# A one-core decoder layer: in the first half of the u side, who adds the two halves, who sums the look-up, and how many raw weight buffers there are

## The chip, the cores and the metric

The kernel runs on 1 of the cores of one Trainium2 chip. The metric is device microseconds of an execution, the median of three runs. A profiled execution of the same program gives the trace; its span is the time from the first to the last instruction.

## The reference, cut to what matters

One layer, float32: a mixer of two attention branches, then a PEER feed-forward part, in which each token picks 16 of 16384 single-neuron experts for each of 8 heads.

```python
q = (hf @ wq).reshape(T, PEER_HEADS, 2, PEER_QDIM // 2)          # T = 256 tokens, D = 1024
s = jnp.einsum('thpd,hpnd->thpn', q, subkeys)                    # 128 keys in each of two halves
s1, i1 = lax.top_k(s[:, :, 0], 16); s2, i2 = lax.top_k(s[:, :, 1], 16)
cand = s1[..., :, None] + s2[..., None, :]                       # 256 sums for a token and a head
top_s, pos = lax.top_k(cand, 16)
idx = take_along_axis(i1 * 128 + i2, pos); w = softmax(top_s)
act = gelu(einsum('cd,chkd->chk', x_c, u[idx]))                  # u, v: 16384 x 1024
out = einsum('chk,chkd->cd', w * act, v[idx])
```

The kernel does not gather rows of `u` for most tokens: it multiplies all of `u` with 224 of the 256 tokens (the other 32 are gathered), takes the GELU of everything, and multiplies it later with a weight that is zero for experts that were not picked.

## The kernel before, in words

**Slots.** All large weights pass through one list, `order`, of 128x1024 float32 blocks of 512 KB. Block k is used in slot k. `U0` is written here for the first of the 128 u blocks, and "slot n" below is the n-th of them, counted from 0. The function `slot` writes the instructions of one slot in this order: the fetches (`fetch`, issued by SyncE, SP in the profile), the routing steps of this slot (`first`, below), what stands in the list `early`, the high part of block k + 2 (`whi`, a copy on ScalarE to a shorter float format, L200), its low part (`wlo`, raw minus high, on VectorE, L204), what stands in `late`, the list `pre`, the list `after`, and last the matmuls of block k. Each engine runs its own instructions in just this order; semaphores hold the engines together. There are three buffers each for raw, high and low blocks: the raw buffer of a block comes free when its low part has been taken, and the next transfer into it starts then, whatever slot the other engines are in; a high or low buffer comes free when the matmuls that read it are done.

**The u side, first half.** A pair e is slots 2e and 2e + 1. For pairs 0 to 29 (`WIDE`), `use_both` runs 8 matmuls of 448 columns (high part of the weights times the high and the low part of the tokens, side by side) and 8 of 224 (low part of the weights times the high part of the tokens, added to the second half). The first slot of a pair goes to a bank `pj` of PSUM, the second to a bank `pT`, two buffers of each. So the bank of pair e is wanted again by pair e + 2. The result of a slot is the sum of the two 224-column halves of its bank. Before, ScalarE copies both halves out (`qt`, L1260), GpSimd adds them into `G` (L1261), and ScalarE takes the GELU of the pair one slot later (L1263). In pairs 30 and 31 all matmuls go to one half each and ScalarE takes the GELU straight out of the bank.

**The routing steps.** In the same slots VectorE picks the top 16 keys, builds the candidates, picks again, and looks the chosen indices up. `steps` is a list of steps with a price in us by the author; `advance(PACE)` adds PACE to a credit at the start of a slot and runs steps while the credit lasts. A pick for one head is a step of 0.85 (`top16_a`) and one of 1.25 (`top16_b`). The look-up of one token block b and key half k compares (`look_eq`, L1066), multiplies with a table that ScalarE writes (`look_tab`, L1063; `look_mul`, L1070) and sums 16 products in four halving additions (`look_sum`, L1075; `look_end`, L1080 and L1081). `soft_exp` (L1012) needs another ScalarE table than the GELU. By the prices, block 0 is looked up in slots 28 to 38 before, and block 1 in slots 49 to 59. `tables(1)` in slot 63 transposes the results of block 1 on TensorE; it stands ahead of the matmuls of that slot.

Of the kernel before, what the change touches and what calls it, by code (L numbers as in the profile page):

```python
# [9 lines left out]
F32 = mybir.dt.float32  # L10
# [9 lines left out]
P = 128  # L20
# [8 lines left out]
EPS = 1e-6  # L29
CAND = 112  # L30
TG = 8
PACE = 1.03
WARM = 15
WSCALE = 32768.0
XCUT = ((0, 2), (2, 5), (5, 8))
# [106 lines left out]
def body(tc, nc, a):  # L142
# [31 lines left out]
    order += [a["u_t"][k] for k in range(P)] + [a["v_n"][k] for k in range(P)]  # L174
    raws, parts, at = {}, {}, [0]
    spares, V0, ahead = [], len(order) - P, [3]

    def fetch(k):
        if k in raws or k >= len(order):
            return  # L180
        ap = order[k]
        spare = spares and (k - V0) % (3 + SPARE) >= 3
        t = (spares[0] if spare else stream).tile([P, D], F32, name="raw", **({"bufs": SPARE} if spare else {}))
        if len(ap.shape) == 3:
            t = t[:, :ap.shape[1] * ap.shape[2]]
# [56 lines left out]

    def slot(use, first=(), pre=()):
        k = at[0]
        for n in range(2, ahead[0] + 1):
            fetch(k + n)
        for f in first:
            f()
        run(early)
        new = k + 2 not in parts and k + 2 < len(order)  # L250
        if new:
            high(k + 2)[0]()
        if tick in pre:
# [132 lines left out]
        slot(use, first[1], pre[1])  # L386
        to.append(lambda: evac(box[0]))

    def pair_wide(src, pool, name, sums, done=None, pre=((), ()), bufs=2):
        def use(j):  # L390
            def f(hi, lo):
                o = bank("pj")
                wh, wl = (v.rearrange("p (c m) -> p c m", m=P) for v in (hi, lo))
                for c in range(NC):
                    nc.tensor.matmul(o, wh[:, c], flat(src[:, c]), start=(c == 0), stop=False, skip_group_check=True)  # L395
                for c in range(NC):
                    nc.tensor.matmul(o[:, T:], wl[:, c], src[:, c, 0], start=False, stop=(c == NC - 1),  # L397
                                     skip_group_check=True)

                def out():  # L400
                    t = pool.tile([P, 2, T], F32, name=name, bufs=bufs)
                    nc.scalar.activation(t, halves(o), AF.Copy)
                    nc.gpsimd.tensor_tensor(sums()[:, j], t[:, 0], t[:, 1], OP.add)
                    if j and done:
                        after.append(done)
                early.append(out)
            return f

        slot(use(0), (), pre[0])
        slot(use(1), (), pre[1])  # L410
# [661 lines left out]
    def look_sum(b, k):  # L1072
        e = eq[k]
        for n in (8, 4):
            nc.vector.tensor_tensor(e[:, :, 0:n], e[:, :, 0:n], e[:, :, n:2 * n], OP.add)  # L1075

    def look_end(b, k):
        e = eq[k]
        o = ii[b, k] = sel.tile([P, 8, 16], F32, name="idx", bufs=2)
        nc.vector.tensor_tensor(e[:, :, 0:2], e[:, :, 0:2], e[:, :, 2:4], OP.add)  # L1080
        nc.vector.tensor_tensor(o, e[:, :, 0], e[:, :, 1], OP.add)  # L1081

    def tables(b):
        tp = bank("pO")
# [59 lines left out]
    for b in range(2):  # L1144
        steps.append((1.2, cands, b))
        for m in range(4):
            steps += pick(best, b, m)
            if b == 1 and m == 2:
                steps += [(0.3, route), (0.5, tables, 0)]
        steps += [(0.3, soft_sub, b), (0.9, decode, b), (0.1, soft_exp, b), (1.2, choose, b), (0.2, look_idx, b, 0),  # L1150
                  (1.15, look_eq, b, 0), (0.0, look_tab, b, 0), (0.7, soft_div, b), (0.2, look_idx, b, 1),
                  (1.15, look_mul, b, 0),
                  (1.15, look_eq, b, 1), (0.0, look_tab, b, 1), (0.95, look_sum, b, 0), (0.6, look_end, b, 0), (1.15, look_mul, b, 1),
                  (0.95, look_sum, b, 1), (0.6, look_end, b, 1)]
    credit = [0.0]

    def advance(us):
# [51 lines left out]
    for m in range(8):  # L1209
        first, second = [], []  # L1210
        if m:
            if m + 1 < 8:
                first.append(lambda: sub_load(m + 1))
            if m == 1:
                second.append(lambda: spread(rn2[0], rsb))
            second.append(lambda: score(m - 1))
            second.append(lambda: norm_chunk(m - 1))
            if m == 7:
                second.append(lambda: norm_chunk(7))
            if m > 1:  # L1220
                first.append(lambda m=m: advance(1.6 if 2 < m < 6 else 1.3 if m < 7 else 1.0))
                second.append(lambda: advance(0.6 if m in (2, 7) else 1.4 if m < 6 else 1.2))
        if m in (0, 7):
            pair(q_evac(m), bh, bl, ((), ()), (first, second), last=(6, 7) if m == 0 else (), to=late)
        else:
            pair_wide(bboth, sel, "qt", q_sums(m), pre=([begin_norm] + first if m == 1 else first, second), bufs=3)

    spots = {"blocks": 0, "tokens": 0}  # L1230
    gelus = []
    dense = lambda t: t[:, :2 * TD].rearrange("p (j t) -> p j t", j=2)

    def u_pair(e, first=((), ()), pre=((), ())):
        box = []

        def use(hi, lo):
            j = len(box) and 1
            if not box:
                box.append(bank("pj"))  # L1240
            block_t(box[0][:, j * TD:(j + 1) * TD], (hi, lo), ah[:, :, NG:], al[:, :, NG:])
            box.append(0)
# [24 lines left out]
        def evac():
            g = G[e // 32][:, 2 * (e % 32):2 * (e % 32) + 2]
            w = spots["tokens"]
            pu = dense(box[0])  # L1270
            if w:
                t = oh.tile([P, 2, TD], F32, name="gt", bufs=1)
                nc.scalar.activation(t[:, :, :w], pu[:, :, :w], AF.Gelu)
                if w < TD:
                    nc.scalar.activation(g[:, :, w:], pu[:, :, w:], AF.Gelu)
                gd = g[:, :, :w]
                nc.vector.tensor_tensor(gd, gd, t[:, :, :w], OP.mult)
            else:
                nc.scalar.activation(g, pu, AF.Gelu)
            spots["blocks"] += 2  # L1280

        f = use_both if e < WIDE else use
        if gelus:
            after.append(gelus.pop(0))
        slot(f, first[0], pre[0])
        slot(f, first[1], pre[1])
        if e >= WIDE:
            late.append(evac)

    for e in range(32):  # L1290
        pre = ((rows_out,), (io_tables,)) if e == 0 else ((lambda: score(7),), ()) if e == 1 else ((), ())
# [310 lines left out]
```

## Time and profile before

| | before |
|---|---|
| median of 3 runs | 983.15 us (981.8 to 984.39) |
| profiled execution, its own time | 983.56 us |
| its span | 981.8 us |
| busy share of the span | PE 98%, PEld 92%, DVE 83%, ACT 64%, POOL 23% |
| POOL instructions L1261 (the additions of the halves) | 60, 54.5 us |

PE is TensorE's matmuls and PEld its weight loads, DVE is VectorE, ACT ScalarE, POOL GpSimd. Busy PE is no proof of PE at its peak, since the ends of matmuls are modelled; the distance between the starts of slots tells more. A row of busy time by stretch gives the bounds, the length, busy us and (instructions) of PE, PEld, DVE, ACT and POOL, then the granted TensorE clock, the busy share of the DMA engines, and GB/s. The clock is 1.00 of full speed in all stretches that are shown below.

### The profile page before, as it was taken

Reading aid. Unit: us, or ns where it says so; the run is one execution under the profiler, and the core shown is the slowest. Engines: PE = TensorE matmul, PEld = TensorE weight load, DVE = VectorE, ACT = ScalarE, POOL = GpSimd, SP = SyncE. Lnnn points to the kernel's source line nnn. Section 1 sums busy time; section 2 is a strip of 40 time slices with the busy share of each in tenths; the row PEclk is TensorE's granted clock in tenths of the full one; section 3 lists DMA queues with packets and bytes.
Section 4 is the critical chain, followed back from the end, with each engine's and each line's share of the span. In section 5 each row is a group of like instructions: output and inputs, shape, how many; then the busy total and the mean of one; then the engine's idle time right before and its main releaser. Section 6 shows DMA issues by size and latency. Waiting matters only on the chain.

```text
span 981.8 us, 18999 instructions
## 1 busy us (share of the span) xinstructions
PE 961.0 (98%) x7057; PEld 906.7 (92%) x7057; DVE 810.6 (83%) x1474; ACT 629.7 (64%) x1177; POOL 230.3 (23%) x210
## 2 busy tenths in 40 slices
PE   9999999999999999999999999999999999999996
PEld 7888889999898998889999999999999999999995
DVE  6788876876998979895999999878887888888766
ACT  7556555756576787776988888655555555555563
POOL 3011231001223423331011011114432343334200
PEclk9999999999999999999999999999999999999999
DMA  8823434665556755557665655678888888888871
GB/s 265 273 89 106 122 116 129 181 200 173 178 168 209 225 182 190 188 193 256 210 218 186 212 209 211 203 262 315 319 321 295 288 317 320 317 310 311 284 232 44
DMA packets 61564, 216.63 MB, mean 221 GB/s; under 512 B 7136, under 2 KB 8848, under 8 KB 61464
## 3 DMA queue, kind: packets, MB, share of 16 engines
q1 hardware_dynamic: 48352, 174.42, 53.1%
q0 software_dynamic: 11424, 39.16, 10.9%
q10 hardware_dynamic: 1696, 1.84, 0.6%
q8 instruction: 56, 0.92, 0.4%
q14 instruction: 36, 0.29, 0.1%
HBM read 212.34 MB, written 2.52 MB: 219 GB/s over the span
## 4 chain that ended last, share of the span: by engine, by line
PE 73%; DVE 15%; ACT 5%; DMA 4%; issue 2%; ACTq 0%; SPq 0%; DVEq 0%
PE pj L372 22%; PE acc L1403 21%; PE acc L1407 11%; DVE wlo L204 7%; PE pj L395 4%; PE pw L1350 3%; ACT whi L200 2%; DMA raw<-in_u_t 2%; PE pj L397 2%; PE pT L1252 1%; DMA raw<-in_w_t 1%; PE pj L1252 1%; DVE sc L976 1%; PE pS L689 1%; PE pS L528 1%
## 5 line engine op out<-in xcount | busy, mean ns | idle before, releaser
L204 DVE TENSOR_TENSOR wlo<-raw,whi 128x1024 fp32r<-128x1024 f32 (+2 forms) x329 | 401.9, 1223 | 105.6 <-ACT whi L200 104.6
L200 ACT ACTIVATE whi<-raw 128x1024 fp32r<-128x1024 f32 (+2 forms) x329 | 343.4, 1045 | 73.2 <-DMA raw<-in_u_t 28.5
L1403 PE MATMUL acc<-co,whi 128*128 128x448 f32 x1024 | 231.2, 367 | 0.1
L1403 PEld LDWEIGHTS acc<-co,whi 128*128 128x128 f32 x1024 | 182.9, 189 | 11.7 <-issue 0.3
L372 PE MATMUL pj<-both,whi 128*128 128x224 f32 (+1 forms) x1344 | 170.7, 279 | 1.8 <-ACT whi L200 1.2
L372 PEld LDWEIGHTS pj<-both,whi 128*128 128x128 f32 x1344 | 159.2, 191 | 4.6 <-ACT whi L200 1.6
L1314 ACT ACTIVATE co<-G 128x224 fp32r<-128x224 f32 x128 | 50.0, 391 | 141.3 <-PE acc L1407 141.3
L1407 PEld LDWEIGHTS acc<-co,wlo 128*128 128x128 f32 x1024 | 134.8, 191 | 4.2 <-DVE wlo L204 0.8
L1407 PE MATMUL acc<-co,wlo 128*128 128x224 f32 x1024 | 135.2, 273 | 0.5 <-DVE wlo L204 0.5
L1120 POOL DMA_INDIRECT row<-in_u_n,sidx x32 | 57.1, 1784 | 245.0 <-DVE row L1129 238.5
L372 PE MATMUL pj<-both,wlo 128*128 128x224 f32 (+1 forms) x672 | 90.3, 276 | 0.0
L1120 POOL DMA_INDIRECT row<-in_v_n,sidx x32 | 62.3, 1947 | 106.1 <-DVE ysum L1438 90.0
L372 PEld LDWEIGHTS pj<-both,wlo 128*128 128x128 f32 x672 | 82.8, 191 | 0.0
L1261 POOL TENSOR_TENSOR G<-qt 128x224 f32<-128x224 f32 x60 | 54.5, 913 | 92.0 <-ACT qt L1260 92.0
L1338 ACT ACTIVATE onehot<-onehot,wl 128x128 f16<-128x128 f16 x224 | 71.3, 392 | 7.2 <-DVE onehot L1342 7.1
L1315 DVE TENSOR_TENSOR co<-G,co 128x224 fp32r<-128x224 f32 x128 | 50.4, 394 | 17.3 <-ACT co L1314 17.1
L1252 PE MATMUL pT<-both,whi 128*128 128x448 f32 x240 | 54.6, 369 | 2.8 <-ACT whi L200 2.8
L1252 PE MATMUL pj<-both,whi 128*128 128x448 f32 x240 | 54.6, 370 | 2.1 <-ACT whi L200 1.9
L395 PE MATMUL pj<-both,whi 128*128 128x512 f32 x192 | 51.1, 408 | 0.0
L1252 PEld LDWEIGHTS pT<-both,whi 128*128 128x128 f32 x240 | 42.9, 189 | 6.6 <-ACT whi L200 3.7
L1252 PEld LDWEIGHTS pj<-both,whi 128*128 128x128 f32 x240 | 42.9, 189 | 5.6 <-ACT whi L200 2.6
L395 PEld LDWEIGHTS pj<-both,whi 128*128 128x128 f32 x192 | 34.5, 189 | 7.3 <-issue 0.7
(335 smaller groups left out, 1298.2 us busy)
## 6 DMA issues: line engine op xcount, KB each, us to landing
raw<-in_u_t SPq DMA_DIRECT2D x128, 512.0 KB, 3.3
raw<-in_v_n SPq DMA_DIRECT2D x128, 512.0 KB, 4.0
raw<-in_w_m SPq DMA_DIRECT2D x16, 512.0 KB, 3.7
raw<-in_w_q SPq DMA_DIRECT2D x16, 512.0 KB, 3.6
raw<-in_w_t SPq DMA_DIRECT2D x15, 512.0 KB, 4.8
raw<-in_w_b SPq DMA_DIRECT2D x8, 512.0 KB, 3.5
raw<-in_w_o SPq DMA_DIRECT2D x8, 512.0 KB, 3.6
sg<-in_w SPq DMA_DIRECT2D x4, 512.0 KB, 6.5
```

What stands on the lines that cost most here:

```text
L200: return [lambda s=slice(u, min(v, n)): nc.scalar.activation(hi[:, s], raws[k][:, s], AF.Copy) for u, v in cuts]
L204: nc.vector.tensor_tensor(lo[:, cs], raws[k][:, cs], hi[:, cs].bitcast(F32), OP.subtract)
L372: nc.tensor.matmul(out, (wl if v == 2 else wh)[:, c], (l if v == 1 else h)[:, c], start=(i == 0), stop=(i == len(seq) - 1))
L395: nc.tensor.matmul(o, wh[:, c], flat(src[:, c]), start=(c == 0), stop=False, skip_group_check=True)
L1120: nc.gpsimd.indirect_dma_start(rows_of_step(n), None, src, bass.IndirectOffsetOnAxis(ap=sidx[:, n % NG:n % NG + 1], axis=0))
L1252: nc.tensor.matmul(o[:, :2 * TD], wh[:, c], both[:, c, :, NG:], start=(c == 0), stop=False, skip_group_check=True)
L1261: nc.gpsimd.tensor_tensor(g[:, j], t[:, 0], t[:, 1], OP.add)
L1314: nc.scalar.activation(t[:, :TD], g, AF.Copy)
L1315: nc.vector.tensor_tensor(t[:, TD:], g, t[:, :TD].bitcast(F32), OP.subtract)
L1338: nc.scalar.activation(E[:, 1, t], E[:, 1, t], AF.Copy, scale=wl[:, n:n + 1])
L1403: nc.tensor.matmul(acc[c][:, :2 * TD], w[0][:, c * P:(c + 1) * P], coefs[k], start=(k == 0), stop=False, skip_group_check=True)
L1407: nc.tensor.matmul(acc[c][:, small], w[1][:, c * P:(c + 1) * P], coefs[k][:, :TD], start=False, stop=(k == P - 1), skip_group_check=True)
```

## The change

Four things in the first half of the u side. The copies on ScalarE take only the second halves (224 columns of each bank, tile `lowsum`), both at the start of the slot after the pair, and VectorE adds them to the first halves, which it reads out of the banks; the GELU follows in the slot after that. The four additions of a look-up go from VectorE to GpSimd, and are priced 0.05 and 0.05 instead of 0.95 and 0.6. PACE is 0.92 instead of 1.03. From block `U0 + 8` to the end of the half, two blocks of every five go to two further raw buffers, which lie in SBUF that is no longer used (half of `xt`, and `g_wide`), and fetches are written up to five blocks ahead. The tile `qt` of the stage before has two buffers instead of three.

```diff
-PACE = 1.03
+PACE = 0.92
...
+    U0, UM = V0 - P, V0 - P // 2
+    more = []
...
+        other = more and U0 + 8 <= k < UM and (k - U0) % (3 + SPARE) >= 3
+        t = more[(k - U0) % (3 + SPARE) - 3] if other else (spares[0] if spare else stream).tile(...
...
-        for n in range(2, ahead[0] + 1):
-            fetch(k + n)
+        far = 3 + SPARE if U0 + 4 <= k < UM else ahead[0]
+        for n in range(2, far + 1):
+            if n <= 3 or not k < UM <= k + n:
+                fetch(k + n)
...
     def look_sum(b, k):
         e = eq[k]
         for n in (8, 4):
-            nc.vector.tensor_tensor(e[:, :, 0:n], e[:, :, 0:n], e[:, :, n:2 * n], OP.add)
+            nc.gpsimd.tensor_tensor(e[:, :, 0:n], e[:, :, 0:n], e[:, :, n:2 * n], OP.add)
...
-            def out():
-                t = sel.tile([P, 2, T], F32, name="qt", bufs=3)[:, :, :TD]
-                nc.scalar.activation(t, dense(o), AF.Copy)
-                nc.gpsimd.tensor_tensor(g[:, j], t[:, 0], t[:, 1], OP.add)
-                if j:
-                    gelus.append(lambda: nc.scalar.activation(g, g, AF.Gelu))
-                    spots["blocks"] += 2
-            early.append(out)
+        def evac_both():
+            g = G[e // 32][:, 2 * (e % 32):2 * (e % 32) + 2]
+            t = sel.tile([P, 2, TD], F32, name="lowsum", bufs=2)
+            for j in range(2):
+                nc.scalar.activation(t[:, j], box[j][:, TD:2 * TD], AF.Copy)
+
+            def add():
+                for j in range(2):
+                    nc.vector.tensor_tensor(g[:, j], t[:, j], box[j][:, :TD], OP.add)
+                late.append(lambda: nc.scalar.activation(g, g, AF.Gelu))
+            after.append(add)
+            spots["blocks"] += 2
```

On VectorE, slots 1 to 4 of the u side hold this before (`tv`, `ti` and `sc` are the values, indices and scores of a pick; the lines of a program are counted anew in each kernel, so L204 before is L207 after):

```order
L204 TENSOR_TENSOR wlo<-raw,whi 128x1024
L970 MAX tv_2696<-sc 128x8 x2
L972 MAX_INDEX ti_2698<-tv_2696,sc 128x8 x2
L204 TENSOR_TENSOR wlo<-raw,whi 128x1024
L976 MATCH_REPLACE sc<-tv_2696,sc 128x128 x2
L978 MAX tv_2696<-sc 128x8 x2
L980 MAX_INDEX ti_2698<-tv_2696,sc 128x8 x2
L204 TENSOR_TENSOR wlo<-raw,whi 128x1024
```

and this after, the two additions (L1267) behind the low part of the second slot of a row, and no step in slot 3:

```order
L207 TENSOR_TENSOR wlo<-raw,whi 128x1024
L975 MAX tv_2696<-sc 128x8 x2
L977 MAX_INDEX ti_2698<-tv_2696,sc 128x8 x2
L207 TENSOR_TENSOR wlo<-raw,whi 128x1024
L1267 TENSOR_TENSOR G_2674<-lowsum,pj 128x224
L1267 TENSOR_TENSOR G_2674<-lowsum,pT 128x224
L207 TENSOR_TENSOR wlo<-raw,whi 128x1024
```

What moved: in every even slot from 2 on, the bank of the pair before is given back only when VectorE has passed its steps and the low part of the block two slots ahead.

The second place is VectorE in the look-up of block 0, from the product for key half 0 on, before (slots 33 to 36):

```order
L1070 TENSOR_TENSOR sc<-sc 128x2048
L204 TENSOR_TENSOR wlo<-raw,whi 128x1024
L1066 TENSOR_TENSOR sc<-ab_4294,io_2677 128x2048
L204 TENSOR_TENSOR wlo<-raw,whi 128x1024
L1075 TENSOR_TENSOR sc<-sc 128x8x128
L1075 TENSOR_TENSOR sc<-sc 128x8x64
L1080 TENSOR_TENSOR sc<-sc 128x8x32
L1081 TENSOR_TENSOR idx<-sc 128x128
L204 TENSOR_TENSOR wlo<-raw,whi 128x1024
```

and after (slots 37 to 40; the product is L1075 here and the comparison L1071, and `xg` and `g_wide` are the two further raw buffers):

```order
L1075 TENSOR_TENSOR sc<-sc 128x2048
L207 TENSOR_TENSOR wlo<-g_wide,whi 128x1024
L1071 TENSOR_TENSOR sc<-ab_4375,io_2677 128x2048
L207 TENSOR_TENSOR wlo<-raw,whi 128x1024
L1267 TENSOR_TENSOR G_2674<-lowsum,pj 128x224
L1267 TENSOR_TENSOR G_2674<-lowsum,pT 128x224
L1075 TENSOR_TENSOR sc<-sc 128x2048
L207 TENSOR_TENSOR wlo<-raw,whi 128x1024 x2
L1267 TENSOR_TENSOR G_2674<-lowsum,pj 128x224
```

What moved: the four additions are gone from here, and the additions of the halves have come. On GpSimd the 60 additions of the halves are gone, and the look-up of block 0 stands there twice four deep, each addition waiting for the one above it:

```order
L1080 TENSOR_TENSOR sc<-sc 128x8x128
L1080 TENSOR_TENSOR sc<-sc 128x8x64
L1085 TENSOR_TENSOR sc<-sc 128x8x32
L1086 TENSOR_TENSOR idx<-sc 128x128
L1080 TENSOR_TENSOR sc<-sc 128x8x128
L1080 TENSOR_TENSOR sc<-sc 128x8x64
L1085 TENSOR_TENSOR sc<-sc 128x8x32
L1086 TENSOR_TENSOR idx<-sc 128x128
```

What moved: the first of each four starts as soon as VectorE has made the product, without waiting for a slot. By the prices, block 0 is now looked up in slots 31 to 39 and block 1 in slots 52 to 60.

## Rows read from the trace of the kernel before

**Rows 1.** Busy time by stretch; bounds are starts of slots 2, 14, 30, 41, 50, 60.

```profile
280.93:313.67 32.74, 30.87 (x195) 28.98 (x194) 29.17 (x109) 21.68 (x32) 11.91 (x16) 1.00 0.62 203
313.67:354.05 40.38, 40.38 (x258) 38.37 (x257) 35.45 (x130) 29.55 (x46) 16.31 (x16) 1.00 0.70 220
354.05:384.71 30.66, 29.15 (x178) 26.35 (x177) 27.21 (x35) 24.61 (x37) 11.36 (x12) 1.00 0.54 174
384.71:407.74 23.03, 23.03 (x149) 21.90 (x148) 23.03 (x81) 15.58 (x26) 7.71 (x12) 1.00 0.69 228
407.74:437.10 29.36, 26.55 (x162) 23.96 (x161) 22.61 (x30) 25.52 (x41) 10.27 (x11) 1.00 0.49 162
```

**Rows 2.** Timeline of PE: start, us, what, idle before and releaser.

```profile
303.71 1.80 PE L1252 MATMUL pT<-both,whi 128*128 128x448 f32 x8
...
308.10 1.90 PE L1252 MATMUL pj<-both,whi 128*128 128x448 f32 x8 [1.70 <-ACT whi L200]
...
457.21 2.04 PE L372 MATMUL pj<-both,whi 128*128 128x224 f32 x16 [0.86 <-ACT whi L200]
```

**Rows 3.** Chain that ended last: start, us, what; around slot 12.

```profile
301.34 8.52 DMA raw<-in_u_t
309.94 1.07 ACT whi L200
```

**Rows 4.** The same chain in the picks: steps and low parts on DVE.

```profile
291.48 0.53 DVE sc L976 x3
...
292.92 1.12 DVE wlo L204
294.05 0.39 DVE tv L970 x2
...
294.97 1.55 DVE wlo L204
```

**Rows 5.** Timeline of DVE at the end: additions with one input in PSUM.

```profile
966.64 0.39 DVE L1522 TENSOR_TENSOR last<-acc,x 128x224 f32<-128x224 f32 x1
966.95 0.38 DVE L1521 TENSOR_TENSOR x<-x,acc 128x224 f32<-128x224 f32 x1
```

**Rows 6.** Groups by shape, DVE, 275 to 440 us: busy us, mean ns.

```profile
L1075 DVE TENSOR_TENSOR sc<-sc 128x1024 bf16<-128x1024 bf16 x4 | 4.6, 1157 | 0.0
L1075 DVE TENSOR_TENSOR sc<-sc 128x512 bf16<-128x512 bf16 x4 | 2.7, 676 | 0.1
L1080 DVE TENSOR_TENSOR sc<-sc 128x256 bf16<-128x256 bf16 x4 | 2.1, 524 | 0.1
L1081 DVE TENSOR_TENSOR idx<-sc 128x128 f32<-128x128 bf16 x4 | 1.2, 292 | 0.1
```

**Rows 7.** ACT: a chain row (start, us), then groups by shape (busy us, mean ns).

```profile
349.80 0.52 ACT f L1032 x3
...
L1012 ACT ACT_TABLE_LOAD x2 | 2.6, 1283 | 0.0
...
L1063 ACT ACTIVATE sc<-tib 128x1024 bf16<-128x1024 bf16 x8 | 8.0, 1047 | 2.5 <-DVE sc L1070 2.5
...
L1260 ACT ACTIVATE qt<-pT 128x448 f32<-128x448 f32 x30 | 16.1, 536 | 6.9 <-PE pT L1255 4.7 <-POOL G L1261 2.2
```

**Rows 8.** POOL and DVE side by side: two timeline rows, then lines (min/median/max ns).

```profile
102.53 2.12 POOL L706 TENSOR_TENSOR y<-y,ytmp 128x512 f32<-128x512 f32 x1 [1.37 <-DVE ytmp L705]
...
103.44 1.36 DVE L629 TENSOR_SCALAR cleft<-csb,ka 128x256 fp32r<-128x256 f32 x1
...
L1066 DVE TENSOR_TENSOR sc<-ab,io x4: 1210/1213/1221, 360.0 to 425.8; 128x2048 bf16<-128x2048 bf16 x4
...
L1070 DVE TENSOR_TENSOR sc<-sc x4: 1687/1690/1702, 365.5 to 433.2; 128x2048 bf16<-128x2048 bf16 x4
```

**Rows 9.** Lines of POOL: durations, ns min/median/max.

```profile
L1261 POOL TENSOR_TENSOR G<-qt x60: 659/674/3428, 282.4 to 438.2; 128x224 f32<-128x224 f32 x60
...
L706 POOL TENSOR_TENSOR y<-y,ytmp x4: 1282/1707/2128, 99.9 to 137.7; 128x512 f32<-128x512 f32 x4
```

More of the change, by code (lines that the diff above doesn't have):

```diff
@@ L182, in fetch @@
         spare = spares and (k - V0) % (3 + SPARE) >= 3
-        t = (spares[0] if spare else stream).tile([P, D], F32, name="raw", **({"bufs": SPARE} if spare else {}))
+        other = more and U0 + 8 <= k < UM and (k - U0) % (3 + SPARE) >= 3
+        t = more[(k - U0) % (3 + SPARE) - 3] if other else (spares[0] if spare else stream).tile([P, D], F32, name="raw", **({"bufs": SPARE} if spare else {}))
         if len(ap.shape) == 3:
@@ L387, in pair, with pair_wide @@
         to.append(lambda: evac(box[0]))
-    def pair_wide(src, pool, name, sums, done=None, pre=((), ()), bufs=2):
+    def pair_wide(src, pool, name, sums, done=None, pre=((), ())):
         def use(j):
@@ L400, in out @@
                 def out():
-                    t = pool.tile([P, 2, T], F32, name=name, bufs=bufs)
+                    t = pool.tile([P, 2, T], F32, name=name, bufs=2)
                     nc.scalar.activation(t, halves(o), AF.Copy)
@@ L1079, in look_end @@
         o = ii[b, k] = sel.tile([P, 8, 16], F32, name="idx", bufs=2)
-        nc.vector.tensor_tensor(e[:, :, 0:2], e[:, :, 0:2], e[:, :, 2:4], OP.add)
-        nc.vector.tensor_tensor(o, e[:, :, 0], e[:, :, 1], OP.add)
+        nc.gpsimd.tensor_tensor(e[:, :, 0:2], e[:, :, 0:2], e[:, :, 2:4], OP.add)
+        nc.gpsimd.tensor_tensor(o, e[:, :, 0], e[:, :, 1], OP.add)
     def tables(b):
@@ L1152, in body @@
                   (1.15, look_mul, b, 0),
-                  (1.15, look_eq, b, 1), (0.0, look_tab, b, 1), (0.95, look_sum, b, 0), (0.6, look_end, b, 0), (1.15, look_mul, b, 1),
-                  (0.95, look_sum, b, 1), (0.6, look_end, b, 1)]
+                  (1.15, look_eq, b, 1), (0.0, look_tab, b, 1), (0.05, look_sum, b, 0), (0.05, look_end, b, 0), (1.15, look_mul, b, 1),
+                  (0.05, look_sum, b, 1), (0.05, look_end, b, 1)]
     credit = [0.0]
@@ L1225, in body @@
         else:
-            pair_wide(bboth, sel, "qt", q_sums(m), pre=([begin_norm] + first if m == 1 else first, second), bufs=3)
+            pair_wide(bboth, sel, "qt", q_sums(m), pre=([begin_norm] + first if m == 1 else first, second))
     spots = {"blocks": 0, "tokens": 0}
-    gelus = []
     dense = lambda t: t[:, :2 * TD].rearrange("p (j t) -> p j t", j=2)
@@ L1242, in use @@
             box.append(0)
-        g = G[e // 32][:, 2 * (e % 32):2 * (e % 32) + 2]
         def use_both(hi, lo):
-            j = len(box)
-            o = bank("pT" if j else "pj")
+            o = bank("pT" if box else "pj")
             box.append(o)
@@ L1282, in u_pair @@
         f = use_both if e < WIDE else use
-        if gelus:
-            after.append(gelus.pop(0))
         slot(f, first[0], pre[0])
         slot(f, first[1], pre[1])
-        if e >= WIDE:
-            late.append(evac)
+        (early if e < WIDE else late).append(evac_both if e < WIDE else evac)
     for e in range(32):
+        if e == 2:
+            more += [flat(xt[:, 0:4]), g_wide]
         pre = ((rows_out,), (io_tables,)) if e == 0 else ((lambda: score(7),), ()) if e == 1 else ((), ())
```

## The prediction

> **What bounds the kernel now.** I read first the busy time by stretch, cut at the starts of slots [rows 1], then the timeline of TensorE around the gaps [rows 2], and last the chain of waits there [rows 3]. In the second stretch 16 slots take 40.38 us, 2.524 us each, with PE busy throughout: that is the pace which the matmuls set. Against it the first stretch (12 slots) loses 32.74 - 30.29 = 2.45 us, the third (11 slots, the look-up of block 0) 30.66 - 27.76 = 2.90, the fourth (9 slots) 0.31, and the fifth (10 slots, the look-up of block 1) 29.36 - 25.24 = 4.12. So there are 9.8 us to be had in this half, and none beyond it but 0.86 us in slot 67, where PE waits for a high part [rows 2]. The loss of the first stretch is one event: slot 11 starts at 303.71 and slot 12 at 308.10, since a transfer that is 2 to 3 slots ahead at best took 8.52 us [rows 3]. In the look-ups the columns of DVE and ACT say more than PE's: DVE is busy for 27.21 of 30.66 us and ACT for 25.52 of 29.36; in the picks between them DVE is busy for all 23.03 us [rows 1]. What the reader is to see: PE sets the pace, VectorE is just behind it, and the look-ups, where VectorE and ScalarE wait for each other, are where time is lost.
>
> **Raw buffers.** With five buffers a transfer may start when the low part five blocks back is taken instead of three back, two slots or 5.0 us sooner, and the stall of slots 12 and 13 came from a transfer about 5 us too slow for its place. I take the whole 2.45 us. At the end of the half the buffers rotate so that the blocks of slots 64 to 66 start a slot sooner, which should free slot 67: 0.86 us. Term -3.3; at least -2.4, if only the first holds.
>
> **Additions on VectorE in the picks.** A step of 0.85 takes 294.97 - 294.05 less the low part before it; between the starts of the rows the low part stands for 1.13 us, the short step for 0.92 and the long one for 1.44 [rows 4]. So 2.1 credits cost 2.36 us, 1.12 us a credit. Before, a slot gives VectorE 1.03 x 1.12 + 1.13 = 2.29 us. An addition with one input in a bank stands for 0.31 us when the next follows at once and for 0.39 alone [rows 5]; there is one a slot. After: 0.92 x 1.12 + 1.13 + 0.31 = 2.47 us, or 2.55 at the upper end. Against 2.524 of PE that is 0 to +1.0 us over 37 slots of picks. Term +0.3. GpSimd's 60 additions, which lay beside other work, go for nothing.
>
> What this does to the slack matters more. In slot 6 the low part starts at 294.97 and ends near 296.5 [rows 4], while slot 7 starts about 293.6 (280.93 and five slots): VectorE is 2.9 us late. Before, it wins back 0.23 us a slot; at slot 28, which starts near 349.0, ScalarE already copies the decoded positions at 349.80 [rows 7], only 0.8 us late. After, it wins back 0.05 us a slot, so it comes to the look-up in slot 31 about 2 us late. And the bank of pair e is given back behind the low part of its slot, so the same lateness stands between TensorE and the start of pair e + 2.
>
> **The look-up of block 0, after.** On ScalarE, from the start of slot 31: 2.0 late, 0.3 for the first decoding, 0.9 for five copies (three take 0.52 [rows 7]), a high part of 1.07 [rows 3], GELU and exponential about 0.9 (an estimate), a table load of 1.28, two copies of 0.37 (half of 0.536 at least, all of it at most [rows 7]), a high part of 1.07: 8.3 us, where slot 34 needs it at 7.57. Then index, high part, table load, GELU, two table copies of 1.05 [rows 7], two half copies, high part: 7.0 us for two slots of 5.05. Together 2.7 us lost. Then the product (slot 37) must be followed by the table for the second key half (2.0), two copies (0.74), the high part (1.07), the low part (1.13) and one addition (0.31), 5.25 us, before slot 40 can start. VectorE is then between 1.0 us late (copies, high part, low part and additions, 3.56, less a slot) and 3.3 (nothing won back); with 2.7, and 1.3 for the product, slot 40 comes 1.7 us late and slot 38 about 0.5: 2.2.
>
> **The sums on GpSimd.** No sum of this kind ran there. By the additions of 224 (0.659) and 512 elements (1.282) [rows 9], 2.16 ns an element: 2.39, 1.28, 0.73 and 0.45 us, 4.85 for a chain; half of that, or twice, are the bounds, since these are 2-byte numbers. Two rows say that GpSimd and VectorE shut each other out. An operation of VectorE's on 256 elements took 1.36 us, more than the low part's 1.13 for 1024, and ended at 104.80, just after GpSimd's 2.12 us had ended at 104.65 [rows 8]. And all four products took 1.69 us where the comparison of the same size took 1.21 [rows 8]; in each case an addition of GpSimd's had been waiting and went first. But GpSimd also lost: one of its 0.66 us additions took 3.43 [rows 9]. The Trainium skill, "SBUF — State Buffer", section "Who interferes with whom", states that a VectorE operation with two inputs in SBUF and a GpSimd operation that reads SBUF exclude each other for a whole instruction, whoever issues first. By that rule, each chain would cost its length; by the 3.43 us, VectorE can go on past a waiting GpSimd and pay less. I take what lies between: behind the low part the first sum (2.39) gets in before the comparison, and VectorE loses 2.1; in the second chain low parts follow one another, 1.5. In block 1 the first chain costs 2.1; the second runs in slots 60 to 63, where no additions stand on VectorE, and only `tables(1)` waits for it, 0 to 3.7, taken as 0.9.
>
> What goes: 10.6 us of sums from VectorE (4.6 + 2.7 + 2.1 + 1.2 [rows 6]). They are left out of the chains above, so nothing is subtracted again.
>
> **Sum.** Look-up of block 0: 2.7 + 2.2 + 2.1 + 1.5 = 8.5 us against 2.90, +5.6. Block 1, where decoding and exponential fall in one slot and VectorE is as late: 1.9 + 1.7 + 2.1 + 0.9 = 6.6 against 4.12, +2.5. With -3.3 and +0.3 that is +5.1. On the profiled execution's own 983.56 (span 981.8) it gives 988.7; the median of the runs is 0.4 lower, so **988.3 us**.
>
> **The rivals.** (A) Faster. VectorE catches up after all, because nothing of GpSimd's gets in its way in the picks, and ScalarE, which has 0.17 us a slot less to copy, never falls behind; the look-ups then lose about 1.5 and 2.0 us. For it: ScalarE has idle time in the picks (29.55 of 40.38 busy [rows 1]), and sums on VectorE are part of today's loss. Against it: 2.47 of 2.524 leaves almost nothing to win back with. It gives -1.4 - 2.1 - 3.3 = -6.8, about 976.4. It decides where an addition costs VectorE under 0.25 us net. (B) No change to be measured: the sums give way on GpSimd, as in the 3.43 us, and the rest holds: 4.9 and 3.6 us in the look-ups, +2.0 - 0.5 + 0.3 - 3.3 = -1.5, 981.7. (C) Every sum shuts VectorE out, 4.2 us a chain (4.85 less what passes under two additions), and `tables(1)` waits 3.7: 4.9 + 8.4 = 13.3 and 3.6 + 4.2 + 3.7 = 11.5 us, +10.4 + 7.4 - 3.0, 998. The page named above would have it so; the products that all lost 0.48 speak for it, the 3.43 us against it.
>
> **How the numbers follow.** The forecast has 0.40 (its own range 985.5 to 993), A 0.29, B 0.20, C 0.11. A range from 977 to 997 leaves out about 0.13 below, the lower half of A, and 0.06 above. A difference of 0.3%, 2.9 us, is about what a measurement of this kernel tells from none. Faster than that: A, 0.29. Within it: most of B and the edge of the forecast, 0.20. Slower: the rest, 0.51.
>
> **What would show it.** Right: no wait of ScalarE for raw blocks around slot 12; VectorE over 95% busy in slots 14 to 30; PE waiting for the additions L1267 or for high parts in slots 33 to 44 and 53 to 60; comparisons or low parts of 2.5 us and more beside a GpSimd sum. Wrong: starts of slots 2.53 us apart through the look-ups, or sums on GpSimd under 1 us. If the picks themselves run at over 2.6 us a slot, an addition costs more than rows 5 show, and the loss is larger and elsewhere.

## The result, and the profile after

Predicted 988.3 us (977 to 997); measured 990.32 us (median of 4, 989.67 to 991.42), against 983.19 us (981.8 to 984.39) for the kernel before on the same chip. The ratio is 1.0076, 95% interval [1.0061, 1.0092]: slower, as forecast, by 7.1 us. The profiled execution took 990.62 us, its span is 988.8.

First the busy time by stretch, cut at the starts of slots 2, 14, 30, 41, 50, 60 and 67 (columns as in [rows 1]):

```profile
279.86:314.24 34.38, 31.17 (x195) 29.11 (x194) 30.25 (x112) 19.85 (x32) 1.61 (x3) 1.00 0.71 239
314.24:354.62 40.38, 40.38 (x259) 38.35 (x257) 39.87 (x142) 25.34 (x40) 0.00 (x0) 1.00 0.66 216
354.62:386.52 31.90, 28.43 (x178) 26.57 (x177) 26.71 (x51) 24.67 (x42) 9.03 (x5) 1.00 0.53 170
386.52:411.50 24.98, 23.48 (x149) 22.04 (x148) 24.98 (x78) 13.78 (x26) 6.75 (x6) 1.00 0.57 191
411.50:441.04 29.54, 25.62 (x163) 24.05 (x161) 25.09 (x49) 22.52 (x38) 7.93 (x5) 1.00 0.50 162
441.04:464.49 23.45, 21.00 (x172) 20.77 (x172) 16.34 (x16) 13.02 (x25) 11.96 (x9) 0.93 0.65 220
```

Against [rows 1]: the picks (second row) run at the same 40.38 us, with VectorE busy for 39.87 of them. The first stretch, where five buffers should have saved 2.4 us, is 1.6 us longer. The look-up of block 0 (third row) is 1.2 longer, the stretch behind it 1.95, the look-up of block 1 0.2, and the seven slots behind that 3.3 (20.11 before: from 437.10 [rows 1] to 457.21 [rows 2]). These are 8.4 us. The half starts 1.1 us sooner (279.86 for 280.93), ahead of the new steps of the u side, and 0.3 are won behind slot 67 (524.3 us to the end of the span for 524.6); so the span is 7.0 longer.

The timeline of TensorE shows where the slots wait:

```profile
294.67 1.90 PE L1253 MATMUL pT<-both,whi 128*128 128x448 f32 x8 [1.77 <-ACT whi L203]
298.88 1.46 PE L1253 MATMUL pj<-both,whi 128*128 128x448 f32 x6 [1.43 <-DVE G L1267]
...
383.94 1.86 PE L1253 MATMUL pj<-both,whi 128*128 128x448 f32 x8 [1.64 <-DVE G L1267]
...
423.58 1.86 PE L1253 MATMUL pj<-both,whi 128*128 128x448 f32 x8 [1.82 <-DVE G L1267]
441.04 2.02 PE L377 MATMUL pj<-both,whi 128*128 128x224 f32 x16 [2.10 <-DVE G L1267]
451.98 0.33 PE L1091 MATMUL pO<-ident,idx 128*128 128x128 f32 x1 [2.44 <-POOL idx L1086]
```

Three kinds of wait: a raw block with what follows from it (slots 7 and 8, at 294.67 and 298.88; the stall of slots 12 and 13 is gone), the additions L1267 that give the bank back (slots 34, 36, 40, 42, 44, 54 and 60, of which three are shown), and in slot 63 the index that GpSimd's last sum makes.

The chain of waits around slot 7 (start, us, what), and GpSimd's issue of the copy that sends 32 token rows to all groups (`tokens_out`):

```profile
284.67 8.49 DMA raw<-in_u_t
...
293.56 1.06 ACT whi L203
...
294.64 1.23 DVE wlo L207
```

```profile
283.70 0.61 POOL L1115 DMA_DIRECT2D xhs<-xhd  x1 [2.36 <-DMA xhd<-xhw]
```

Before, the same copy stands 14 us later, since GpSimd had the additions of the halves ahead of it in its queue:

```profile
297.64 0.64 POOL L1110 DMA_DIRECT2D xhs<-xhd  x1
```

The 8.52 us transfer of [rows 3], at 301.34, came behind it. So the slow transfer has moved along with the copy; whether the copy is its cause is what e2, e4 and e5 ask.

VectorE in the look-up of block 0, from its product for key half 0 on:

```profile
375.95 1.22 DVE L1075 TENSOR_TENSOR sc<-sc 128x2048 bf16<-128x2048 bf16 x1
377.09 1.22 DVE L207 TENSOR_TENSOR wlo<-g_wide,whi 128x1024 fp32r<-128x1024 f32 x1
378.22 3.17 DVE L1071 TENSOR_TENSOR sc<-ab,io 128x2048 bf16<-128x2048 bf16 x1
381.31 2.18 DVE L207 TENSOR_TENSOR wlo<-raw,whi 128x1024 fp32r<-128x1024 f32 x1
...
385.15 4.53 DVE L207 TENSOR_TENSOR wlo<-raw,whi 128x1024 fp32r<-128x1024 f32 x2
```

and GpSimd beside it:

```profile
377.26 5.15 POOL L1080 TENSOR_TENSOR sc<-sc 128x1024 bf16<-128x1024 bf16 x2 [92.95 <-DVE sc L1075]
...
385.47 5.22 POOL L1080 TENSOR_TENSOR sc<-sc 128x1024 bf16<-128x1024 bf16 x2
```

The comparison of 1.21 us [rows 8] stands for 3.17, two low parts for 4.53 instead of 2.3, and the bank that slot 40 waits for is free 1.64 us late.

Last the end of the half by stretch: slot 62 with the wait at its end, then slots 63 and 64 (the clock is third from the end):

```profile
446.46:452.06 5.60, 3.15 (x29) 2.92 (x28) 5.18 (x3) 2.02 (x3) 5.37 (x5) 1.00 0.38 117
452.06:456.08 4.02, 4.02 (x25) 4.02 (x26) 0.29 (x1) 0.94 (x3) 2.42 (x3) 0.67 0.90 324
456.08:459.12 3.04, 3.04 (x25) 3.04 (x25) 1.28 (x2) 2.18 (x3) 0.00 (x0) 0.88 0.91 333
```

Behind the wait the granted clock is 0.67 and 0.88 of full speed: part of each slot ran at 1.2 GHz instead of 2.4. Slots 63 and 64 take 7.06 us, where the two slots behind them take 5.37 (459.12 to 464.49).

### The profile page after: what moved, and what is told of

It reads as the page before. It is cut to its first block, busy times and chain, and to the rows that moved or that the text cites. A ratio compares the mean times of both kernels' runs of the same rounds, so it can differ in the third digit from the quotient of the medians.

```text
span 988.8 us, 18941 instructions
## 1 busy us (share of the span) xinstructions
PE 961.7 (97%) x7057; PEld 908.7 (92%) x7057; DVE 822.3 (83%) x1518; ACT 619.3 (63%) x1177; POOL 207.1 (21%) x166
## 3 DMA queue, kind: packets, MB, share of 16 engines
HBM read 212.34 MB, written 2.52 MB: 217 GB/s over the span
## 4 chain that ended last, share of the span: by engine, by line
PE 83%; DVE 10%; ACT 3%; issue 1%; DMA 1%; POOL 1%; SPq 0%; DVEq 0%; ACTq 0%; POOLq 0%
PE pj L377 25%; PE acc L1407 21%; PE acc L1411 11%; PE pj L400 4%; DVE wlo L207 4%; PE pj L1253 4%; PE pT L1253 3%; PE pw L1354 3%; PE pj L402 2%; PE pj L1256 2%; PE pT L1256 2%; ACT whi L203 1%; PE pS L694 1%; DMA raw<-in_u_t 1%; PE pS L533 1%
## 5 line engine op out<-in xcount | busy, mean ns | idle before, releaser
L207 DVE TENSOR_TENSOR wlo<-raw,whi 128x1024 fp32r<-128x1024 f32 (+2 forms) x306 | 376.2, 1231 | 90.7 <-ACT whi L203 89.8
L203 ACT ACTIVATE whi<-raw 128x1024 fp32r<-128x1024 f32 (+2 forms) x306 | 318.6, 1044 | 56.2 <-PE pj L377 28.9
L1080 POOL TENSOR_TENSOR sc<-sc 128x1024 bf16<-128x1024 bf16 (+1 forms) x8 | 20.4, 2548 | 114.9 <-DVE sc L1075 114.6
```

What stands on the lines that cost most here:

```text
L203: return [lambda s=slice(u, min(v, n)): nc.scalar.activation(hi[:, s], raws[k][:, s], AF.Copy) for u, v in cuts]
L207: nc.vector.tensor_tensor(lo[:, cs], raws[k][:, cs], hi[:, cs].bitcast(F32), OP.subtract)
```

## The experiments

The theories: the sums on GpSimd cost most, because GpSimd and VectorE shut each other out and because `tables(1)` waits for the last chain; and the buffers gain nothing because the copy now starts early. The rivals: that the additions on VectorE are what costs; and that the burst of fetches with which five buffers begin makes the stall. Each run was timed beside the kernel before on its own chip: 982.3 to 982.8 us on the three chips of the runs, 983.19 on the chip of the changed kernel. So times of different runs compare to about 1 us.

Losses in the table are the length of a stretch less 2.524 us for each of its slots, from the starts of slots in each trace; the last column is the plain length. A trace is of one execution: that of e4 is the fastest of six (985.1 to 989.76 us), and a stretch in which the granted clock fell, as told at the end, is longer by that.

| kernel | us | slots 2-14 | 30-41 | 41-50 | 50-60 | 60-67, us |
|---|---|---|---|---|---|---|
| before | 983.2 | 2.45 | 2.90 | 0.31 | 4.12 | 20.11 |
| after | 990.3 | 4.09 | 4.14 | 2.26 | 4.30 | 23.45 |
| e1: after, sums on VectorE | 984.25 | 4.41 | 2.96 | 1.11 | 3.61 | 19.60 |
| e2: before, five buffers | 979.07 | 0.06 | 2.89 | 0.32 | 4.12 | 19.08 |
| e3: before, sums on GpSimd | 994.29 | 2.77 | 1.81 | 6.55 | 2.27 | 26.66 |
| e4: after, copy later | 986.86 | 0.73 | 4.17 | 2.26 | 4.81 | 21.83 |
| e5: after, three buffers | 990.66 | 4.20 | 4.17 | 2.26 | 4.91 | 24.90 |
| e6: after, last chain on VectorE | 987.15 | 3.99 | 4.16 | 2.27 | 4.30 | 19.86 |
| e7: e1 and e4 together | 979.65 | 0.99 | 2.94 | 1.11 | 3.10 | 19.63 |
| e8: e2, halves on VectorE in look-ups | 978.13 | 0.06 | 3.46 | 0.32 | 3.04 | 19.09 |
| e9: e5 with e1, idle sums on GpSimd | 995.6 | 4.28 | 8.30 | 1.95 | 6.22 | 22.48 |
| e10: e8 in block 1 alone | 977.56 | 0.07 | 2.91 | 0.32 | 3.16 | 19.08 |

### e1: the sums on VectorE again

```diff
-            nc.gpsimd.tensor_tensor(e[:, :, 0:n], e[:, :, 0:n], e[:, :, n:2 * n], OP.add)
+            nc.vector.tensor_tensor(e[:, :, 0:n], e[:, :, 0:n], e[:, :, n:2 * n], OP.add)
...
-        nc.gpsimd.tensor_tensor(e[:, :, 0:2], e[:, :, 0:2], e[:, :, 2:4], OP.add)
-        nc.gpsimd.tensor_tensor(o, e[:, :, 0], e[:, :, 1], OP.add)
+        nc.vector.tensor_tensor(e[:, :, 0:2], e[:, :, 0:2], e[:, :, 2:4], OP.add)
+        nc.vector.tensor_tensor(o, e[:, :, 0], e[:, :, 1], OP.add)
```

> The changed kernel, with the four look-up sums issued on VectorE again; their prices in the step list, the pace and their place in the order stay as in the changed kernel. Theory (the sums on GpSimd cost through the exclusion of VectorE and through the late last chain): the comparisons of 3.17 us and low parts of 4.53 us for two go back to about 1.2 each, slot 63 no longer waits 2.4 us for idx, and the clock does not fall in slots 63 and 64; VectorE gets 10.6 us of sums back, of which the exclusion cost about as much. About 4 to 6 us faster than the changed kernel, 985 +-1.5. Rival (VectorE is the bound of the look-ups because of the additions): the 10.6 us of sums stand on its path, the waits for the additions grow, and the kernel takes 992 or more.

984.25 us, ratio to before 1.0014 [1.0005, 1.0023]: 6.1 us faster than the changed kernel. Groups by shape on VectorE, 275 to 470 us (busy us, mean ns):

```profile
L1071 DVE TENSOR_TENSOR sc<-ab,io 128x2048 bf16<-128x2048 bf16 x4 | 4.9, 1216 | 0.0
L1080 DVE TENSOR_TENSOR sc<-sc 128x1024 bf16<-128x1024 bf16 x4 | 2.7, 687 | 0.1
L1080 DVE TENSOR_TENSOR sc<-sc 128x512 bf16<-128x512 bf16 x4 | 1.7, 427 | 0.1
L1085 DVE TENSOR_TENSOR sc<-sc 128x256 bf16<-128x256 bf16 x4 | 1.2, 292 | 0.1
L1086 DVE TENSOR_TENSOR idx<-sc 128x128 f32<-128x128 bf16 x4 | 1.2, 291 | 0.1
```

The 16 sums take VectorE 6.8 us in all; in [rows 6] they took 10.6, with GpSimd's additions running beside them. And in the changed kernel the four comparisons alone stand for 8.8 us instead of 4.9, and 58 low parts have means of 1.33 to 1.35 us instead of 1.21 to 1.22, 7 us more in all:

```profile
L207 DVE TENSOR_TENSOR wlo<-raw,whi 128x1024 fp32r<-128x1024 f32 x46 | 61.2, 1334 | 12.1 <-ACT whi L203 12.0
L207 DVE TENSOR_TENSOR wlo<-xg,whi 128x1024 fp32r<-128x1024 f32 x12 | 16.2, 1349 | 2.5 <-ACT whi L203 2.4
...
L1071 DVE TENSOR_TENSOR sc<-ab,io 128x2048 bf16<-128x2048 bf16 x4 | 8.8, 2193 | 0.0
```

So VectorE was relieved of 6.8 us, and its comparisons and low parts stood for some 11 longer.

### e2: the five raw buffers alone

The edits of `fetch`, `slot`, `U0`, `UM` and `more` from the change, put into the kernel before.

> The kernel before, with the five raw buffers alone (additions of halves on GpSimd, sums on VectorE). Theory (the stall of slots 7 and 8 in the changed kernel is there because GpSimd's queue reaches the copy of the tokens 14 us sooner): the copy still starts near 297.6, when five buffers are in use, so slots 12 and 13 lose nothing and slot 67 too; 2.5 to 3.3 us faster than before, 980.3 +-1. Rival (the burst of three fetches when the two new buffers are taken up makes the stall by itself): slots 7 and 8 lose about 4 us here as well, and the time is 983 to 985.

979.07 us, ratio 0.9962 [0.9949, 0.9976]: 3.3 us faster, the size that the prediction gave this term. The first stretch loses nothing, and slots 60 to 67 are 1.0 us shorter:

```profile
279.20:309.55 30.35, 30.35 (x195) 28.83 (x194) 30.35 (x109) 22.00 (x32) 13.56 (x16) 1.00 0.75 255
...
432.98:452.06 19.08, 19.08 (x173) 19.08 (x172) 13.52 (x15) 12.61 (x23) 4.34 (x4) 1.00 0.78 260
```

The copy stands at 295.91 here, behind GpSimd's additions:

```profile
295.91 0.64 POOL L1115 DMA_DIRECT2D xhs<-xhd  x1
```

### e4: the copy of the tokens later

```diff
     def tokens_out():
-        nc.gpsimd.dma_start(xhs.rearrange("(g t) d -> g t d", t=NG), xhd[None].to_broadcast([NR, NG, D]))
+        nc.sync.dma_start(xhs.rearrange("(g t) d -> g t d", t=NG), xhd[None].to_broadcast([NR, NG, D]))
```

> The changed kernel, with the copy of the tokens (L1115) issued from SyncE's queue behind the fetch of block 13 instead of from GpSimd's, where nothing holds it. Theory (the early copy slows the fetches while only three buffers are in use): the copy starts near 298 us, no raw block of slots 7 and 8 takes over 5 us, and the 4.1 us lost in slots 2 to 14 go: about 986.3. Rival (the burst of fetches itself is the cause): slots 7 and 8 still lose about 4 us and the time stays at 990.

986.86 us, ratio 1.0044 [1.0028, 1.0060]: 3.5 us faster than the changed kernel. On SyncE's queue the burst of fetches begins at 284.02 with the first of the two further buffers (`xg`), 1.03 us before its place in the changed kernel, as slot 2 does (278.81 for 279.86); the copy follows at 294.42, and slots 2 to 14 lose 0.73 us instead of 4.09:

```profile
284.02 0.42 SPq L192 DMA_DIRECT2D xg<-in_u_t  x1
...
294.42 0.72 SPq L1115 DMA_DIRECT2D xhs<-xhd  x1
```

### e5: the early copy with three buffers

The changed kernel without the edits of e2.

> The changed kernel with three raw buffers, as before: no burst of three fetches, but the copy of the tokens still issued early, at about 283 us, by GpSimd. Theory (the copy by itself slows the fetches, whatever is in flight): a raw block of slots 6 to 9 still comes about 2 to 4 us late, slots 12 and 13 lose nothing, slot 67 loses its 0.9 again, and the time is 990 to 992. Rival (only copy and burst together are too much): no stall in slots 2 to 14 at all, 986 to 988.

990.66 us, ratio 1.0091 [1.0076, 1.0107]. No burst, the copy at 282.71, and the stall is there in slots 7 and 8 as in the changed kernel, behind a transfer of the same length (chain of waits):

```profile
283.74 8.59 DMA raw<-in_u_t
```

With e4 this settles it for the changed kernel: the early copy from GpSimd's queue makes the stall, with the burst or without. Where five buffers are in use when the copy starts, there is none, from SyncE's queue (e4) or from GpSimd's (e2); an early copy from SyncE's queue was not run. That the stall of slots 12 and 13 before came from the copy too fits this. In e3, again with three buffers, the copy stands at 295.77, a block's transfer takes 8.84 us from 296.93 on, and slot 12 starts 2.6 us late. But no run took the copy out of such a kernel. One expectation failed: slot 67 does not lose 0.9 us again here, it starts 2.68 us behind slot 66. And in the changed kernel the five buffers, worth 3.3 us by themselves, are worth nothing that the times resolve (990.3 and 990.7).

### e6: the last chain on VectorE

```diff
-            nc.gpsimd.tensor_tensor(e[:, :, 0:n], e[:, :, 0:n], e[:, :, n:2 * n], OP.add)
+            (nc.vector if (b, k) == (1, 1) else nc.gpsimd).tensor_tensor(e[:, :, 0:n], e[:, :, 0:n], e[:, :, n:2 * n], OP.add)
```

and likewise for the two additions of `look_end`.

> The changed kernel with the last of the four chains of sums (block 1, second key half) on VectorE, the other three on GpSimd. Theory (tables(1) waits 2.4 us for the GpSimd chain, and the clock falls behind that wait): slot 63 starts 2.7 us after slot 62, slots 63 and 64 keep their full clock: 3 to 4.5 us faster than the changed kernel, 986 to 987. Rival (the chain is late because VectorE is late with its product, so the wait stays, and the clock falls at another stall): less than 1.5 us faster, 989 or more.

987.15 us, ratio 1.0058 [1.0044, 1.0072]: 3.2 us faster than the changed kernel by the medians, but only 1.8 by the ratios, whose intervals overlap. The traces are clearer: slots 60 to 67 take 19.86 us instead of 23.45, and no other stretch of the table moves by more than 0.1. Slot 63 starts 3.00 us behind slot 62 (447.06 to 450.06), and the clock in it stays at 1.00:

```profile
450.06:452.81 2.75, 2.75 (x27) 2.75 (x26) 1.43 (x2) 1.10 (x4) 2.02 (x2) 1.00 0.84 289
```

So that chain costs 3.6 us by the traces, about half of what the sums cost: from e1 to the changed kernel slots 30 to 60 lose 3.0 us more, and slots 60 to 67 are 3.85 longer.

### e9: sums that nobody waits for

In the changed kernel with three raw buffers and the sums on VectorE, GpSimd does four additions of the same sizes a chain beside them (`look_sum` calls `idle_sum` first), into a tile that nobody reads.

```diff
+    def idle_sum(k, b):
+        e = eq[k]
+        d = g_wide.bitcast(BF).rearrange("p (h a k) -> p h a k", h=8, a=16)
+        nc.gpsimd.tensor_tensor(d[:, :, 0:8], e[:, :, 8:16], e[:, :, 8:16], OP.add)
+        nc.gpsimd.tensor_tensor(d[:, :, 0:4], d[:, :, 0:4], d[:, :, 4:8], OP.add)
+        nc.gpsimd.tensor_tensor(d[:, :, 0:2], d[:, :, 0:2], d[:, :, 2:4], OP.add)
+        nc.gpsimd.tensor_tensor(d[:, :, 8], d[:, :, 0], d[:, :, 1], OP.add)
```

> The changed kernel with three raw buffers and its sums on VectorE, and beside them the same four additions a chain on GpSimd as work that nobody waits for: they read a half of the comparison that nothing writes, and write into a tile that this half does not use. Their results are thrown away. So GpSimd is on no path, and only its sharing with VectorE can cost. Theory (exclusion): the comparison behind the first product takes 3.2 us again, low parts 2.2 us and more, and the stretches 30-41, 41-50 and 50-60 lose 2 to 5 us more than the 2.96, 1.11 and 3.61 of the kernel with the sums on VectorE alone; slot 63 keeps its 2.7 to 3.0. Rival (sums on GpSimd cost because of who waits for them): the comparison takes 1.2 us and the stretches lose what they lost there, within 1 us in all.

995.6 us, ratio 1.0135 [1.0116, 1.0155]. On VectorE, at the comparison and the sums that stand beside the first of them:

```profile
377.43 1.22 DVE L204 TENSOR_TENSOR wlo<-raw,whi 128x1024 fp32r<-128x1024 f32 x1
378.56 2.92 DVE L1066 TENSOR_TENSOR sc<-ab,io 128x2048 bf16<-128x2048 bf16 x1
381.40 2.46 DVE L1084 TENSOR_TENSOR sc<-sc 128x1024 bf16<-128x1024 bf16 x2
```

and GpSimd:

```profile
377.60 2.80 POOL L1075 TENSOR_TENSOR g_wide<-sc 128x1024 bf16<-128x1024 bf16 x1 [93.31 <-DVE sc L1070]
...
387.65 2.31 POOL L1075 TENSOR_TENSOR g_wide<-sc 128x1024 bf16<-128x1024 bf16 x1 [3.51 <-DVE sc L1070]
390.04 1.23 POOL L1076 TENSOR_TENSOR g_wide<-g_wide 128x512 bf16<-128x512 bf16 x1
```

GpSimd's sum ends at 380.40 and the comparison 1.08 us behind it, about its own length of 1.22; it takes 2.92 us. VectorE's own sums, with GpSimd's additions beside them, take 15.3 us where they take 6.8 in e1. The low parts, expected at 2.2 us and more, are not longer (mean 1.216 us): in this kernel VectorE's sums stand where low parts do in the changed one. The three stretches of the look-ups lose 8.8 us more than in e1 (16.47 less 7.68), above the 2 to 5 expected. Part of that is the slower clock behind the waits: slot 40 takes 4.81 us at a clock of 0.50, and slot 41 4.10 at 0.83; but e1 pays for one such slot too (slot 54, 4.17 at 0.59). So the two engines' sharing costs by itself, with no engine waiting for GpSimd's results. That it costs the 6 to 7 us of the change in just the same way is argued from this and the comparisons above.

### e3: the sums on GpSimd, alone

The edits of `look_sum`, `look_end`, the prices and PACE, in the kernel before.

> The kernel before, with the four look-up sums on GpSimd alone (and their prices and the pace as in the changed kernel). Theory (each sum shuts VectorE out for its own length, and tables(1) waits for the last chain): comparisons of about 3.2 us and slot 63 late by 2 to 3 us, 3 to 6 us slower than before, 986 to 989. Rival (the sums off VectorE free it, and only together with the additions of halves on VectorE do they hurt): 2 to 4 us faster than before, 979 to 981.

994.29 us, ratio 1.0117 [1.0098, 1.0135]: 11.95 us slower, where 3 to 6 were expected. GpSimd still has the additions of the halves in its queue, behind the sums, and ScalarE waits for them:

```profile
384.54 0.58 ACT L1263 ACTIVATE G<-G 128x448 f32<-128x448 f32 x1 [3.15 <-POOL G L1261]
...
392.14 0.55 ACT L1260 ACTIVATE qt<-pT 128x448 f32<-128x448 f32 x1 [5.65 <-POOL G L1261]
```

With ScalarE held for 5.65 us no high part is made, and slots 43 and 44 take 6.15 and 4.68 us, the second at a clock of 0.52. `tables(1)` waits 4.67 us, since the last chain stands behind two additions of the halves. By these waits the sums hurt less in the change than alone because the additions had left GpSimd.

### e7, e8, e10: the rest of the account

e7 is the changed kernel with the edits of e1 and e4: five buffers and the halves on VectorE remain, with the new pace and prices, which were not run by themselves.

> The changed kernel without its sums on GpSimd (they are issued on VectorE) and with the copy of the tokens issued from SyncE's queue: what remains of the change is five raw buffers and the halves added on VectorE. If the account is additive (sums -6.1, copy -3.5 on the changed kernel's 990.3): 980.7 +-1.2, which leaves +1.6 for the halves on VectorE beside the five buffers alone. Rival (the halves on VectorE cost what the prediction put on lateness, about +4 in the look-ups once the sums are on VectorE as well): 983 or more.

979.65 us, ratio 0.9973 [0.9964, 0.9982], 0.6 us above the five buffers alone, with intervals that overlap: the halves on VectorE cost nothing that these runs resolve. The three look-up stretches lose 7.15 us, and 7.33 with the halves on GpSimd (e2).

e8 and e10 ask whether the halves do better on VectorE in the look-ups alone.

```diff
+    LOOK = lambda e: 15 <= e < 21 or 25 <= e < WIDE
...
+            if LOOK(e):
+                return
...
+        elif LOOK(e):
+            early.append(evac_both)
```

> The kernel before with five raw buffers, sums on VectorE, and the halves added by VectorE only in the pairs that lie in the two look-ups (15 to 20 and 25 to 29); in all others GpSimd adds them as before. In the look-ups ScalarE ends the waits, and it has 0.17 us a slot less to copy there. Theory (ScalarE is what the look-ups wait for): they lose 1 to 3 us less than the 2.9 and 4.1 of the kernel with five buffers alone, 976.5 to 978. Rival (VectorE, which was busy for 27.2 of 30.7 us there, takes ScalarE's place): 979 to 981, with PE waiting for the additions.

> Five raw buffers, sums on VectorE, halves added by VectorE in the pairs 25 to 29 alone. Of the two look-ups, block 1 lost 1.1 us less with the halves on VectorE (3.04 for 4.12) and block 0 lost 0.6 more (3.46 for 2.89). If each stands for itself: 976.5 to 978, 1 us below the kernel with five buffers alone, which the comparison may not resolve. Rival (the additions only move the wait): 978 to 980.

978.13 us, 0.9962 [0.9948, 0.9976], and 977.56 us (pairs 25 to 29 alone), 0.9949 [0.9934, 0.9964]. In e8 block 0 loses 0.6 more and block 1 1.1 less: 0.5 us in all, where 1 to 3 were expected. In e10 the 1.0 us of block 1 stays. The times do not tell either from e2; e10 has the lowest median of all and beats both kernels of the change.

## Why the prediction was right, and where it was wrong

The kernels before, e2, e7, e4 and after form a chain in which each adds one thing: the buffers -3.3 us, the halves (with pace and prices) +0.6, the sums +7.2, the early copy +3.5, each known to 1 to 2 us. They add up to 8.0 because they are steps from 982.34 to 990.32, which proves nothing by itself; on its own chip the change measured 7.1, since the kernel before took 983.19 there. The prediction had -3.3 for the buffers, +0.3 and +1.5 for the halves (picks, and lateness in the look-ups), 6.6 for the sums, and no copy: +5.1. Its split of halves and sums cannot be set against the runs term by term: its lateness is reckoned with the sums off VectorE and its 6.6 without any relief for that, whereas e7 has the sums on VectorE, so that its 0.6 and the 7.2 behind it are net. Together they are +8.4 forecast and +7.8 measured. The sign and the largest term were right, and what is missing is the 3.5 us of the copy.

- **The step that failed**: "GpSimd's 60 additions, which lay beside other work, go for nothing." They were on no path, but they were what held the copy of `tokens_out` back on GpSimd's queue, from 283.70 to 297.64. With them gone the copy falls where only three raw buffers are in use, and the transfer beside it takes 8.49 us. So "I take the whole 2.45 us" failed too, though the buffers do just that in e2. [Rows 3] showed an 8.52 us transfer, and the prediction never asked what had slowed it; GpSimd's issue at 297.64, in the same trace, is by what e4 and e5 show the likely answer, and the change moved it. The reading was also one block off: that transfer is the one which slot 13 waited for, by 0.18 us. Slot 12 waited for the block before it, whose high part ScalarE could start only at 306.99:

```profile
306.99 1.06 ACT L200 ACTIVATE whi<-raw 128x1024 fp32r<-128x1024 f32 x1 [4.99 <-DMA raw<-in_u_t]
```

- **Raw buffers, -3.3**: right for the buffers alone (e2), slot 67 too; in the changed kernel they bring nothing (e5).
- **The picks, +0.3**: right. Slots 14 to 29 take 2.52 to 2.53 us each, and VectorE is busy for 39.87 of 40.38 us.
- **The lateness of ScalarE and of the banks** (4.9 us in block 0 with 2.90 before, 3.6 in block 1 with 4.12): it started from 2.0 us in slot 31. There ScalarE copies the decoded positions 1.19 us behind the start of the slot (357.14), where the working has 2.3 (2.0 and 0.3 for the first decoding), so its start was 1.1 us too late. How much that is worth further on cannot be said, since no run leaves the sums out. The waits for L1267 are there, in the slots forecast (34 to 44, 54, 60), but with the sums on VectorE they only take the place of waits for high and low parts: 7.15 us lost in e7, 7.33 in e2.

```profile
358.33 0.31 ACT L1037 ACTIVATE f<-hi 128x128 f32<-128x128 uint32 x1 [2.21 <-DVE hi L1031]
```

- **The sums**: 6.6 forecast with no relief for VectorE, 6.1 (e1) or 7.2 (e4 against e7) measured net of it, so that the numbers agree in part by luck; and they were wrongly shared out. `tables(1)` was taken at 0.9 us; it waits 2.44, and with the slow clock behind it the last chain costs 3.2 to 3.6 (e6). The other three chains then cost 3 to 4 net, where 5.7 stood without the relief. The durations on GpSimd were good: 2.39 and 1.28 us estimated, 2.31 and 1.23 where little was in their way (e9).
- **The rule**: the Trainium skill, "SBUF — State Buffer", section "Who interferes with whom", has a VectorE operation with two inputs in SBUF and a GpSimd operation that reads SBUF exclude each other for whole instructions. The traces agree for single instructions: the comparison that waits out the 2.80 us sum, the low parts of 2.2 us. For a chain the measured price is lower than the length of its additions. By e9 VectorE loses 3.4 us in the comparisons and 8.5 in its own sums (15.3 less 6.8, over the 16), about 3 us a chain, where rival C took 4.2 by the rule and the prediction 1.5 to 2.1.
- **The rivals**: A needed nothing of GpSimd's to stand in VectorE's way, and B needed GpSimd to give way; VectorE was relieved of 6.8 us and lost more (e1, e9). C had both mechanisms right, and its price of 3.7 for `tables(1)` was near what the last chain cost with the slow clock; it counted every chain in full and came out 8 us too high.

## What to carry to other kernels

Work that is off the path may still set the time of what stands behind it in its queue: before taking it away, list the transfers issued behind it and where they will now land. Give an engine's work to another only after asking whether the two can run side by side; between VectorE and GpSimd here, a sum moved away cost VectorE more than the sum itself (6.8 us given away, some 11 lost to longer instructions). And when a slow transfer explains a stall, look for what slowed it before adding buffers against it.

## What was not expected of the hardware

The granted clock did not follow from the length of the stall ahead of it and TensorE's busy time in it. In the changed kernel slot 53 with its wait takes 4.51 us with TensorE busy for 2.69, and the clock stays at 1.00 behind it; it falls behind the wait of slot 62 (3.15 busy of 5.60), to 0.67:

```profile
419.07:423.58 4.51, 2.69 (x19) 2.41 (x17) 1.67 (x3) 4.48 (x7) 0.00 (x0) 1.00 0.25 90
423.58:426.16 2.58, 2.58 (x16) 2.46 (x17) 2.58 (x9) 2.57 (x6) 0.00 (x0) 1.00 0.61 203
```

In e4 the same two stalls have the same lengths, and it is the other way round: 0.60 behind the first, 1.00 behind the second.

```profile
414.68:419.18 4.50, 2.69 (x18) 2.41 (x17) 1.67 (x3) 4.47 (x7) 0.00 (x0) 1.00 0.24 92
419.18:423.32 4.14, 4.14 (x17) 3.88 (x17) 3.98 (x11) 4.13 (x8) 0.00 (x0) 0.60 0.50 162
...
442.59:448.19 5.60, 3.14 (x29) 2.90 (x28) 5.18 (x3) 2.01 (x3) 5.37 (x5) 1.00 0.41 148
448.19:450.95 2.76, 2.76 (x25) 2.76 (x26) 0.29 (x1) 0.94 (x3) 2.15 (x3) 1.00 0.84 284
```

Each of these falls cost about 1.6 us. Between slots 30 and 67 the clock fell once in the traces of the changed kernel, of e1 and of e4, and not at all in that of e7, whose slot 53 has the same stall as that of e1 (4.50 us, 2.69 busy). One fall is about what the price of the sums from e7 to e4 (7.2) has over that from e1 to the changed kernel (6.1). So a stall of this size carries a risk of the slower clock, and which of them pays it stays open; so does how the copy comes to stretch one block's transfer from SyncE's queue to 8.5 us, which no run here took apart.
